# The mLSTM's full-precision products become three rounded passes each, its first decay weights are made earlier, and the local branch's rounded weights come by casting transfers

## The chip, the core and the metric

The kernel runs on one core of one Trainium2 chip. The core has five engines with an instruction queue each: TensorE (PE, matrix products; its loads of the stationary operand are listed as PEld), VectorE (DVE), ScalarE (ACT), GpSimd (POOL) and SyncE (SP). SP and POOL also issue the transfers (DMA) between the chip's memory and the core's on-chip buffers. The engines run side by side and wait for each other through semaphores.

Some results are kept in memory for later: gd (gates), god (the sigmoid of the output gates) and xk and s, into which transfers add.

The metric is the device time of one execution in microseconds (us). The kernel before takes 880.09 us, the median of three runs (879.93 to 880.3).

## The reference, cut to what matters

One decoder layer for 512 tokens of width 1024, in float32:

```python
h = rmsnorm(x, norm_mix_g)
proj = h @ w_in
qk_ml, v_ml, o_ml, if_pre, q_sw, k_sw, v_sw, g_a, g_b = split(proj)
qk_ml = silu(causal_depthwise_conv(qk_ml, conv_qk))
q_ml, k_ml = split(qk_ml)                    # 4 heads, 128 wide; q_ml is scaled by 128 ** -0.5
ig, lf = gates[..., :4], log_sigmoid(gates[..., 4:])
h_ml = mlstm_chunkwise(q_ml, k_ml, v_ml, ig, lf)      # values 256 wide
y_a = sigmoid(o_ml) * (rmsnorm_per_head(h_ml) * mlstm_norm_g)
y_b = swa_with_sinks(q_sw, k_sw, v_sw, sinks)         # 16 query heads, 4 key heads, window 128
merged = sigmoid(g_a) * (y_a @ w_branch_a) + sigmoid(g_b) * (y_b @ w_branch_b)
x = x + merged @ w_out
x = x + square(relu(rmsnorm(x, norm_mlp_g) @ w_up)) @ w_down
gate = sigmoid(rmsnorm(x, norm_ple_g) @ w_ple_gate)
x = x + gate * (p @ w_ple_proj)
return rmsnorm(x, final_norm_g)
```

The reference walks the mLSTM in chunks of 64 tokens. The kernel computes the same in one piece for each head. With b the running sum of lf and m the running maximum that keeps the exponentials in range, a token t takes from an earlier token s the weight (q_t . k_s) exp(b_t - b_s + i_s - m_t). Its numerator is the sum of these weights times v_s, its denominator the sum of the weights alone, which is found as one more column of ones behind the values.

## The kernel before, in words

**Rounded pairs.** Nearly all products are made from pairs. A float32 operand is split in a rounded half (tag wh for weights, written by an ACT cast, L137) and a remainder (wl, by a DVE subtraction, L138). Three products of halves then stand for one of full precision: high x high, high x low, low x high (`pairs`). They are issued by `chain` at L171. In the trace such products have the type f32 as the full-precision ones do, which are the exception in this kernel and are made at other lines, among them the mLSTM's scores (L819) and its output (L831).

**Weights.** `load_raw` (L152) fetches 512 KB of a weight matrix by a transfer that SP issues, into one of four wr buffers. `load_w` splits them into one of four wh and one of four wl buffers. A buffer of a tag is used in rotation: the split of a weight waits until PE has finished the weight four before it. The other pools rotate in the same way: "act" has 34 tiles of 128x512, "lm" has 4 tiles of 128x1024, "big" has 2 tiles of 128x4096, and the banks that PE writes to come as two of each tag (psg, pst, psa).

**Order.** A scheduler of the framework places the instructions of each engine, from dependencies and its own costs; `tc.issue_after` pins some of them behind a given instruction. The numbers behind names (wh_828, gg_866) are those that the scheduler's listing gives to tiles. They differ between the two kernels for the same tile.

**The stages around the change.** The front of the program forms the normalised input, the projections of the window attention, and then the mLSTM's values (`by_tokens(w_vml, ...)`) and output gates (`by_tokens(w_o, ...)`). The scheme of `by_tokens` is one of seven products of half-size blocks in place of eight; sums of weight blocks (wr, wq; L458, L462) and sums of results (L507, L510) are made beside it by ACT and DVE. `put_v` writes the values to the four tiles vm (L521, L523). Beside these products run the gates of the mLSTM: ig and fg, lf = log sigmoid, the running maximum mst (a scan, L546) and running sums fl (L549), rr = fl - mst (L551, sent to memory and read back as rows across all partitions), gg (L558, L560) and em = exp(-mst) (L562, which follows a load of ACT's table of functions). PE then turns gg and em from rows into columns (gc) by transposes at L572 and L574.

Much later, behind the window attention, `qk_proj(7)` makes the last q and k projection, and `silu` finishes the q and k of the four heads. The stage that the change rewrites then goes through the heads: `branch_b(h)` multiplies the window attention's result yb by a block of w_branch_b (24 products at L171; these blocks are called w_b[0] to w_b[7]), `ml_decay` makes the next head's exponentials (dg by DVE, ten exponentials by ACT at L802 into four tiles dm), `ml_out` forms the output of a head (L831, ten blocks of 128x128 against 257 columns) with copies hs (L834) and hd (L835) out of the banks, and `ml_scores` the next head's scores (L819, blocks of 512, 384, 256 and 128 columns), which DVE multiplies by dm (L823). `ml_norm` normalises, and `ya_of` turns the result and splits it into ya, which w_branch_a multiplies next. w_b[4] to w_b[7] alternate with `ya_of`.

## Time and profile before

| what | value |
|---|---|
| median of three runs | 880.09 us (879.93 to 880.3) |
| the profiled execution's own time | 879.82 us |
| its span | 878.0 us |
| PE busy | 866.8 us (99%), 4372 instructions |
| DVE busy | 657.2 us (75%), 966 instructions |
| ACT busy | 483.5 us (55%), 803 instructions |
| POOL busy | 34.1 us (4%), 58 instructions |
| PE's share of the chain that ended last | 90% |

The span runs from the first to the last instruction that the profile shows, and the execution's own time holds some 1.8 us more. In the view in order of time, a row gives a start in the span, a duration, the engine, the line, the operation with output and inputs, and how many instructions of one kind it puts together; products overlap in the pipeline, so starts, and not durations, tell what one costs. The row of a stretch gives the busy time of PE, PEld, DVE, ACT and POOL with the number of instructions, then the granted clock, the share of time in which transfers ran, and GB/s. The order of the program's rows, shown under the change, gives no times.

### The profile page before, as it was taken

The page shows a single profiled execution, that of the slowest core. Times are in us where ns is not written, and L with a number is a line of the kernel's source. Part 1 is how long each engine was busy: PE and PEld are TensorE (multiplying, and loading weights), DVE is VectorE, ACT ScalarE, POOL GpSimd, SP SyncE. Part 2 cuts the span into 40 slices and gives each one's busy share as a digit, 9 for nine tenths or more (in the row PEclk, how much of TensorE's full clock was granted, in tenths as well). Part 3 has the DMA queues.
Part 4 walks back from the last instruction along what each step waited for, and adds up shares of the span by engine and source line. Part 5 has one row for each costly group of instructions (what it writes and reads, how often), then busy time and mean ns, then how long its engine had stood idle before and what let it go on. Part 6 is the DMA issues. An engine that isn't in the chain of part 4 may idle for free.

```text
span 878.0 us, 11545 instructions
## 1 busy us (share of the span) xinstructions
PE 866.8 (99%) x4372; PEld 725.6 (83%) x4372; DVE 657.2 (75%) x966; ACT 483.5 (55%) x803; POOL 34.1 (4%) x58
## 2 busy tenths in 40 slices
PE   8999999999999999999999999999999999999996
PEld 7888889998777777788888888888888888888886
DVE  6999887875789876665896669756956794698557
ACT  6684554544676768743344665356435634564843
POOL 1111010000000000000020000000000000020000
PEclk9999999999999999999999999999999999999999
DMA  7765244435122162274244612530352054125302
GB/s 266 211 180 186 73 150 169 165 111 196 52 73 72 49 199 88 97 240 144 72 75 145 236 49 71 197 106 10 124 185 75 1 186 149 49 52 141 121 0 96
DMA packets 32793, 106.74 MB, mean 122 GB/s; under 512 B 4573, under 2 KB 4573, under 8 KB 32738
## 3 DMA queue, kind: packets, MB, share of 16 engines
q1 hardware_dynamic: 27570, 93.15, 31.2%
q0 software_dynamic: 5024, 12.59, 5.9%
q8 instruction: 34, 0.56, 0.3%
q10 hardware_dynamic: 144, 0.26, 0.1%
q14 instruction: 21, 0.17, 0.1%
HBM read 91.30 MB, written 8.40 MB: 114 GB/s over the span
## 4 chain that ended last, share of the span: by engine, by line
PE 90%; DVE 4%; ACT 3%; DMA 2%; issue 1%; SPq 0%; ACTq 0%; DVEq 0%
PE psg L171 50%; PE psp L171 23%; PE psa L171 7%; PE pst L171 4%; PE psa L831 1%; PE pst L747 1%; DVE wl L138 1%; DMA wr<-in_w_vsif 1%; ACT lm L712 1%; PE psa L819 1%; PE psa L689 1%; PE psa L690 1%; ACT wh L137 0%; DMA wr<-in_w_gb 0%; PE psp L980 0%
## 5 line engine op out<-in xcount | busy, mean ns | idle before, releaser
L137 ACT CAST wh<-wr 128x1024 fp32r<-128x1024 f32 x138 | 144.8, 1051 | 180.3 <-PE psg L171 74.8
L138 DVE TENSOR_TENSOR wl<-wr,wh 128x1024 fp32r<-128x1024 f32 x138 | 167.8, 1219 | 85.9 <-ACT wh L137 84.6
L171 PE MATMUL psg<-x,wh 128*128 128x512 f32 x512 | 157.7, 389 | 0.0
L171 PE MATMUL psp<-wh,uf 128*128 128x512 f32 x448 | 138.6, 389 | 0.0
L171 PEld LDWEIGHTS psg<-x,wh 128*128 128x128 f32 x512 | 96.0, 188 | 19.9
L171 PE MATMUL psg<-x,wl 128*128 128x512 f32 x256 | 99.6, 389 | 0.0
L171 PEld LDWEIGHTS psp<-wh,uf 128*128 128x128 f32 x448 | 84.1, 188 | 17.5
L171 PE MATMUL psp<-wl,uf 128*128 128x512 f32 x224 | 87.2, 389 | 0.0
L171 PE MATMUL psg<-h,wh 128*128 128x512 f32 x256 | 81.1, 395 | 0.7 <-DVE rc L715 0.7
L137 ACT CAST wh<-wd 128x1024 fp32r<-128x1024 f32 x44 | 46.2, 1052 | 54.0 <-PE psp L171 21.9
L138 DVE TENSOR_TENSOR wl<-wd,wh 128x1024 fp32r<-128x1024 f32 x44 | 53.1, 1217 | 14.7 <-ACT wh L137 14.5
L171 PEld LDWEIGHTS psg<-x,wl 128*128 128x128 f32 x256 | 48.0, 188 | 10.0
L171 PEld LDWEIGHTS psg<-h,wh 128*128 128x128 f32 x256 | 47.0, 188 | 11.2 <-issue 1.6
L171 PE MATMUL psg<-h,wl 128*128 128x512 f32 x128 | 50.5, 395 | 0.0
L138 DVE TENSOR_TENSOR uf<-F,uf 128x1792 fp32r<-128x1792 f32 (+2 forms) x20 | 33.0, 1652 | 21.8 <-ACT uf L137 21.8
L171 PEld LDWEIGHTS psp<-wl,uf 128*128 128x128 f32 x224 | 42.0, 188 | 8.7
L171 PE MATMUL psg<-yb,wh 128*128 128x512 f32 x128 | 41.3, 402 | 0.1
L171 PE MATMUL psg<-ya,wh 128*128 128x512 f32 x128 | 39.5, 390 | 0.0
L137 ACT CAST uf<-F 128x1792 fp32r<-128x1792 f32 (+2 forms) x20 | 27.9, 1396 | 20.5 <-DVE F L1133 20.4
L1157 DVE SCALAR_TENSOR_TENSOR xk<-psp,r,xk 128x512 f32<-128x512 f32 x48 | 33.7, 744 | 5.5 <-PE psp L171 5.2
L171 PE MATMUL psg<-hS,wh 128*128 128x256 f32 x192 | 35.6, 284 | 0.0
L171 PE MATMUL psa<-h,wh 128*128 128x256 f32 x192 | 35.3, 285 | 0.2 <-ACT p L625 0.2
(322 smaller groups left out, 1745.6 us busy)
## 6 DMA issues: line engine op xcount, KB each, us to landing
wr<-in_w_up SPq DMA_DIRECT2D x32, 512.0 KB, 3.3
wd<-in_w_down SPq DMA_DIRECT2D x24, 512.0 KB, 3.7
wr<-in_w_qsw SPq DMA_DIRECT2D x8, 512.0 KB, 4.3
gd<-gr POOLq DMA_DIRECT2D x8, 512.0 KB, 3.7
wr<-in_w_qkml SPq DMA_DIRECT2D x8, 512.0 KB, 3.2
wr<-in_w_b SPq DMA_DIRECT2D x8, 512.0 KB, 3.2
gl<-gd SPq DMA_DIRECT2D x8, 512.0 KB, 3.4
wr<-in_w_a SPq DMA_DIRECT2D x8, 512.0 KB, 4.4
```

The source lines that it names most:

```text
L137: A.copy(dst[0], src)
L138: last_low[0] = V.tensor_sub(dst[1], src, r32(dst[0]))
L171: last_mm[0] = T.matmul(ps, l, r, start=first and i == 0, stop=last and i == len(ops) - 1, skip_group_check=parts)
L689: T.matmul(o, q[:, n * P : (n + 1) * P], kk[kp][ab][:, k0 : k0 + 256], start=True, stop=False)
L690: T.matmul(o, q[:, n * P : (n + 1) * P], kl[kp][ab][:, k0 : k0 + 256], start=False, stop=True)
L712: A.activation(lm3[:, g, :], lm3[:, g, :], AF.Exp, bias=nmx[:, g : g + 1], scale=0.125, accum_out=sm[:, g : g + 1])
L747: T.matmul(o[HALF[ab], :], v[:, c : c + 64], w[:, ab * 512 : (ab + 1) * 512], start=j == 0, stop=j == len(terms) - 1)
L819: T.matmul(psc, qk[4 + h][:, n0 : n0 + P], qk[h][:, n0:], start=True, stop=True, skip_group_check=True)
L831: last_mm[0] = T.matmul(pn[:, t % 2, : DV + 1], wT[s][:, t * P : (t + 1) * P], vm[s][:, h, :], start=s == 0, stop=s == t, skip_group_check ...
L1157: V.scalar_tensor_tensor(o, ps[:, t, :], r2[:, 2 * toks + t : 2 * toks + t + 1], o, ALU.mult, ALU.add)
```

## The change

Four edits are made together.

1. Scores and output products of the mLSTM are made from rounded pairs. q and k of each head are split (`qk_parts`) into slots of the two big tiles that later hold ya (`spare`); the weights wT, now packed into three tiles dm, are multiplied by the scores and split too. vm becomes a rounded tile with 258 columns a head, whose two columns of ones ACT writes. `put_v` also makes the values' remainders vl by a DVE subtraction and sends them to memory (vld) by a POOL transfer; SP reads a head's remainders back into an "lm" tile before its output. The score block of the last 128 keys is formed with 256 columns, of which 128 are used. Where a result of `by_tokens` needs a sum before it is a value, the sum is now made into its own tile (L530), then cast to vm by ACT and subtracted (L532).
2. `ml_decay(0)` stands ahead of `qk_proj(7)`, and only head 0's `silu` stands ahead of its scores; the other heads' follow them.
3. The rounded half of w_b comes straight from memory by a transfer that POOL issues and that casts on the way (L161). SP still fetches the plain block, and DVE still subtracts (L162). ACT no longer casts these eight blocks.
4. Two blocks of w_b stand ahead of head 0's output, one more between head 2's output and head 3's scores, and one each with `ya_of(0)` and `ya_of(2)`.

```diff
     def tk(n):
-        return tp_.tile([P, NH * (DV + 1)], F32, tag="tk", bufs=4, name=nm(n))
+        return tp_.tile([P, NH * (DV + 2)], F32, tag="tk", bufs=4, name=nm(n))
...
-    def load_w(src, n, dims, raw=None):
+    def load_w(src, n, dims, raw=None, cast=False):
...
-        split(parts, raw[:, :n])
+        if cast:
+            nc.gpsimd.dma_start(out=parts[0], in_=src)
+            last_low[0] = V.tensor_sub(parts[1], raw[:, :n], r32(parts[0]))
+        else:
+            split(parts, raw[:, :n])
...
-        t = tk("vm").rearrange("p (h d) -> p h d", h=NH)
-        G.memset(t[:, :, DV : DV + 1], 1.0)
+        t = tp_.tile([P, NH * (DV + 2)], F32R, tag="tk", bufs=4, name=nm("vm")).rearrange("p (h d) -> p h d", h=NH)
+        A.copy(t[:, :, DV:], ones[:, : 2 * NH].rearrange("p (h d) -> p h d", h=NH))
         vm.append(t)
+    vld = dp.tile([P, NH, NT, DV], F32, name="vld")
...
     def put_v(m, nh, ps, k):
         o = vm[m][:, 2 * nh : 2 * nh + 2, :DV]
-        src = ps.rearrange("p (h d) -> p h d", h=2)
+        two = lambda t: t.rearrange("p (h d) -> p h d", h=2)
+        low = act_r("vl")
         if k is None:
-            A.copy(o, src)
+            A.copy(o, two(ps))
+            V.tensor_sub(two(low), two(ps), r32(o))
         else:
-            V.tensor_add(o, src, k.rearrange("p (h d) -> p h d", h=2))
+            V.tensor_add(k, ps, k)
+            A.copy(o, two(k))
+            V.tensor_sub(two(low), two(k), r32(o))
+        nc.gpsimd.dma_start(out=vld[:, 2 * nh : 2 * nh + 2, m, :], in_=two(r32(low)))
...
-    qk_proj(7)
-
-    for h in range(NH):
-        silu(h)
-        silu(4 + h)
-
+    ya_parts, ya = big_hl("ya")
+    turn = [0]
+    def spare():
+        k = turn[0] % KT
+        turn[0] += 1
+        return [t[:, k, :] for t in ya_parts]
+
+    def qk_parts(h):
+        for i in (h, 4 + h):
+            hl = spare()
+            split(hl, qk[i])
+            qk[i] = hl
...
+        dm = [act_f("dm") for _ in range(3)]
+        wT = [dm[0], dm[1][:, :384], dm[2][:, :256], dm[2][:, 256:384]]
...
-        banks = [two[:, :512], two[:, 512:], one, two[:, 512:]]
-        at = [0, 0, 0, 384]
-        for s in (0, 1, 3, 2):
-            n0 = s * P
-            psc = banks[s][:, at[s] : at[s] + S - n0]
-            T.matmul(psc, qk[4 + h][:, n0 : n0 + P], qk[h][:, n0:], start=True, stop=True, skip_group_check=True)
+        psc = [two[:, :512], two[:, 512:896], one[:, :256], one[:, 256:]]
+        q, k = qk[h], qk[4 + h]
         for s in range(NT):
-            n0 = s * P
-            dm = wts[h][s]
-            V.tensor_mul(dm[:, n0:], banks[s][:, at[s] : at[s] + S - n0], dm[:, n0:])
+            n0 = min(s, 2) * P
+            ops = pairs([t[:, s * P : (s + 1) * P] for t in k], [t[:, n0:] for t in q])
+            for j, (l, r) in enumerate(ops):
+                T.matmul(psc[s], l, r, start=j == 0, stop=j == 2, skip_group_check=True)
+        dm, wT = wts[h]
+        hl = []
+        for j, n in enumerate((512, 384, 384)):
+            for s in ((0,), (1,), (2, 3))[j]:
+                V.tensor_mul(wT[s], psc[s][:, P:] if s == 3 else psc[s], wT[s])
+            hl.append([t[:, :n] for t in spare()])
+            split(hl[j], dm[j][:, :n])
+        wts[h] = hl + [[t[:, 256:] for t in hl[2]]]
...
+        low = sp.tile([P, NT, DV], F32R, tag="lm", bufs=LMB, name=nm("vl"))
+        nc.sync.dma_start(out=r32(low), in_=vld[:, h])
...
-                    last_mm[0] = T.matmul(
-                        pn[:, t % 2, : DV + 1], wT[s][:, t * P : (t + 1) * P], vm[s][:, h, :], start=s == 0, stop=s == t, skip_group_check=True
-                    )
+                    hi, lo = [q[:, (t - s) * P : (t - s + 1) * P] for q in wT[s]]
+                    o = pn[:, t % 2, : DV + 2]
+                    T.matmul(o, hi, vm[s][:, h, :], start=s == 0, stop=False, skip_group_check=True)
+                    T.matmul(o[:, :DV], hi, low[:, s, :], start=False, stop=False, skip_group_check=True)
+                    last_mm[0] = T.matmul(o, lo, vm[s][:, h, :], start=False, stop=s == t, skip_group_check=True)
...
-        mm_T(ps, load_w(w_b[i], KT * P, KT), yb)
+        mm_T(ps, load_w(w_b[i], KT * P, KT, cast=True), yb)
...
     ml_decay(0)
+    qk_proj(7)
+    silu(0)
+    silu(4)
+    qk_parts(0)
     ml_scores(0)
+    for h in range(1, NH):
+        silu(h)
+        silu(4 + h)
     rds = []
+    todo = list(range(KT))
     for h in range(NH):
-        branch_b(h)
+        for _ in range(1 if h else 2):
+            branch_b(todo.pop(0))
         if h + 1 < NH:
             ml_decay(h + 1)
+            qk_parts(h + 1)
         with tc.issue_after(last_mm[0].ins):
             rds.append(ml_out(h))
         if h + 1 < NH:
+            if h == 2:
+                branch_b(todo.pop(0))
             with tc.issue_after(last_mm[0].ins):
                 ml_scores(h + 1)
...
     for h in range(NH):
-        branch_b(NH + h)
+        if h % 2 == 0:
+            branch_b(todo.pop(0))
         ya_of(h)
```

Three places in the new order are spoken of below.

The first is in the front of the program, on PE: the transposes of the gates, gg (L572) and em (L574) into a psa bank. Before, they stand between the last product of wh_828 and the first of wh_929; wl_829 is the remainder of wh_828, and h the stationary or moving halves of the input:

```order
L171 MATMUL psa_563<-wl_829,h_158 128x512
L171 MATMUL psa_563<-wh_828,h_159 128x512
L572 MATMUL psa_538<-ident,gg_866 128x4
L574 MATMUL psa_538<-ident,em_877 128x4
L572 MATMUL psa_538<-ident,gg_867 128x4 x2
L574 MATMUL psa_538<-ident,em_877 128x4
L572 MATMUL psa_538<-ident,gg_868 128x4 x3
L574 MATMUL psa_538<-ident,em_877 128x4
L572 MATMUL psa_538<-ident,gg_869 128x4 x4
L574 MATMUL psa_538<-ident,em_877 128x4
L171 MATMUL pst_925<-wh_929,h_158 128x512
```

In the changed kernel, PE has there (these lines are L582 and L584 now, and wh_976 is the block of output gates that was wh_828, wh_1000 the one that was wh_929):

```order
L175 MATMUL pst_957<-wh_976,h_159 128x512
L175 MATMUL psg_958<-wh_1039,hS_387 128x512
L175 MATMUL psg_959<-wh_1039,hS_387 128x512
L582 MATMUL psa_539<-ident,gg_897 128x4
L584 MATMUL psa_539<-ident,em_908 128x4
L582 MATMUL psa_539<-ident,gg_898 128x4 x2
L584 MATMUL psa_539<-ident,em_908 128x4
L582 MATMUL psa_539<-ident,gg_899 128x4 x3
L584 MATMUL psa_539<-ident,em_908 128x4
L582 MATMUL psa_539<-ident,gg_900 128x4 x4
L584 MATMUL psa_539<-ident,em_908 128x4
L175 MATMUL pst_956<-wh_1000,h_158 128x512
```

The transposes now stand behind the first two products of another block, wh_1039, and the product that follows them is still one of the input h.

On DVE the operations that feed these transposes stand so in the changed kernel (L530 and L532 are `put_v`, L453 a sum of weight blocks, L556 the scan that makes mst and is printed as SCALAR_TENSOR_TENSOR, L561 rr, L568 the first rows of gg):

```order
L530 TENSOR_TENSOR t_134_711<-psa_564,t_134_711 128x512
L530 TENSOR_TENSOR t_135_713<-psa_564,t_135_713 128x512
L453 TENSOR_TENSOR wr_941<-wq_945,wr_941 128x1024
L532 TENSOR_TENSOR vl_867<-t_134_711,vm_530 128x512
L532 TENSOR_TENSOR vl_872<-t_135_713,vm_532 128x512
L556 SCALAR_TENSOR_TENSOR mst_886<-lf_881,ig_877 4x512
L138 TENSOR_TENSOR wl_1001<-wr_947,wh_1000 128x1024
L561 TENSOR_TENSOR rr_893<-fl_888,mst_886 4x512
L568 TENSOR_TENSOR gg_897<-ig_877,fl_888 4x128
L568 TENSOR_TENSOR gg_898<-ig_877,fl_888 4x128
```

The two remainders vl and the scan stand ahead of the remainder wl_1001, and gg behind it. ACT's casts wh_1000 and wh_1057, of weights too, stand ahead of em in its queue, and em's instruction waits for the transfer of vl_867 too, since the tiles of the act pool rotate. wl_794 is a weight's remainder that DVE makes some 30 instructions earlier.

The second place is on DVE, while PE forms the first products of the values. Before, wl_688, wl_709 and wl_725 are remainders of weights, L462 is a sum of weight blocks, and t_132 and t_133 (L510) are sums of results, which read the banks psg that PE writes next:

```order
L138 TENSOR_TENSOR wl_688<-wr_549,wh_687 128x1024
L462 TENSOR_TENSOR wr_549<-wq_561,wr_549 128x1024
L138 TENSOR_TENSOR wl_709<-wr_547,wh_708 128x1024
L510 TENSOR_TENSOR t_132_704<-psg_566,p_112_600 128x512
L138 TENSOR_TENSOR wl_725<-wr_549,wh_724 128x1024
L510 TENSOR_TENSOR t_133_706<-psg_567,p_113_602 128x512
L138 TENSOR_TENSOR wl_745<-wq_551,wh_744 128x1024
```

In the changed kernel the same tiles are wl_695, wl_716, wl_732, t_134 and t_135:

```order
L528 TENSOR_TENSOR vl_667<-pst_565,vm_534 128x512
L138 TENSOR_TENSOR wl_695<-wr_550,wh_694 128x1024
L528 TENSOR_TENSOR vl_671<-pst_566,vm_536 128x512
L466 TENSOR_TENSOR wr_550<-wq_562,wr_550 128x1024
L138 TENSOR_TENSOR wl_716<-wr_548,wh_715 128x1024
L515 TENSOR_TENSOR t_134_711<-psg_567,p_112_601 128x512
L515 TENSOR_TENSOR t_135_713<-psg_568,p_113_603 128x512
L138 TENSOR_TENSOR wl_732<-wr_550,wh_731 128x1024
```

Two remainders of values (L528, out of the pst banks) now stand among them, ahead of t_134 and t_135, and t_135 stands ahead of the third remainder.

The third place is on DVE in the mLSTM's stage, around head 1's output, in the changed kernel. ya is a slot that holds a half of q, k or the weights, dg and dm belong to a head's weights, wl_4042 is the remainder of the seventh block of w_b, whose rounded half wh_4041 comes by the casting transfer, and hd is the column of denominators of a head:

```order
L891 TENSOR_TENSOR gb_3663<-psg_3632,gl_3664 128x512
L138 TENSOR_TENSOR ya_3359<-dm_3544,ya_3358 128x384
L810 TENSOR_TENSOR dg_3667<-row_912,tri 128x512
L162 TENSOR_TENSOR wl_4042<-wr_4039,wh_4041 128x1024
L843 TENSOR_TENSOR dm_3671<-pst_3735,dm_3671 128x256
L862 COPY hd<-psa_3688 128x2
L843 TENSOR_TENSOR dm_3671<-pst_3735,dm_3671 128x128
L862 COPY hd<-psa_3712 128x2
```

The subtraction for wl_4042 stands ahead of two multiplications by dm and of the first copy of hd; before, the remainders of w_b waited in the same queue for a cast by ACT.

More of the change, by code (lines that the diff above doesn't have):

```diff
@@ L796, in ml_decay @@
         )
-        wT = []
+        dm = [act_f("dm") for _ in range(3)]
+        wT = [dm[0], dm[1][:, :384], dm[2][:, :256], dm[2][:, 256:384]]
         for s in range(NT):
-            dm = act_f("dm")
             for t in range(s, NT):
@@ L802, in ml_decay @@
                 A.activation(
-                    dm[:, t * P : (t + 1) * P],
+                    wT[s][:, (t - s) * P : (t - s + 1) * P],
                     src[:, t * P : (t + 1) * P],
```

4 lines of the change are left out of this document (1 added, 3 removed).

## The prediction

> **What bounds the kernel now.** I read the page first, its shares and the chain that ended last, then the busy time by stretch, then each engine's rows in order of time around the edits.
>
> ```profile
> span 878.0 us, 11545 instructions
> PE 866.8 (99%) x4372; PEld 725.6 (83%) x4372; DVE 657.2 (75%) x966; ACT 483.5 (55%) x803; POOL 34.1 (4%) x58
> PE 90%; DVE 4%; ACT 3%; DMA 2%; issue 1%; SPq 0%; ACTq 0%; DVEq 0%
> ```
>
> TensorE (PE) is busy for 99% of the span and makes 90% of the chain: the time moves only if PE's products get cheaper or PE is made to wait. In the front of the program VectorE (DVE) is as full as PE:
>
> ```profile
> 65.00:70.00 5.00, 5.00 (x24) 4.14 (x23) 5.00 (x8) 2.21 (x3) 0.00 (x0) 1.00 0.95 323
> ...
> 85.00:90.00 5.00, 5.00 (x24) 4.14 (x23) 5.00 (x6) 2.48 (x4) 0.00 (x0) 1.00 0.00 0
> ...
> 100.00:105.00 5.00, 5.00 (x24) 4.14 (x23) 3.26 (x4) 2.10 (x2) 0.00 (x0) 1.00 0.33 102
> ```
>
> The columns are PE, PEld, DVE, ACT, POOL. All five stretches from 65 to 90 us have DVE at 5.00 of 5.00; room returns by 100. So work added to DVE before 90 us has no cover there but the weights prepared ahead.
>
> **1. The products of the mLSTM.** Prices of PE, as starts of rows:
>
> ```profile
> 149.99 0.40 PE L171 MATMUL psg<-hS,wh 128*128 128x256 f32 x2
> 150.23 0.28 PE L171 MATMUL psg<-hS,wl 128*128 128x256 f32 x1
> ...
> 343.76 0.45 PE pst L819 x2
> ...
> 366.75 1.72 PE psa L819 x6
> ...
> 369.85 4.33 PE psa L831 x20
> ...
> 380.55 5.46 PE psg L171 x24
> ```
>
> Rounded products start every 5.46/24 = 0.2275 us at 512 columns, and two of 256 columns take 150.23 - 149.99 = 0.24, so 0.12 each. On the line between them (an estimate) 258 columns cost 0.121 and 384 cost 0.174. Full-precision products show as two records each.
> - Before, a head: scores 1.72 + 0.43, output 4.33, together 6.48; four heads 25.9 us.
> - After, a head: scores 3 x 0.2275 + 3 x 0.174 + 6 x 0.12 = 1.925 (the fourth block is widened to 256 columns); output 10 x (0.121 + 0.120 + 0.121) = 3.62; four heads 22.2 us.
>
> The gain on PE is 3.7 us. [...] Here the loads take as long as this:
>
> ```profile
> L171 PEld LDWEIGHTS psg<-hS,wh x192: 186/192/193, 124.4 to 200.5; 128*128 128x128 f32 x192
> ```
>
> The row's loads of 192 ns stand under products that start every 120 ns, so several overlap. [...]
>
> **2. Waits of that stage.** It runs from w_b[0] to w_b[4]:
>
> ```profile
> 325.23 0.63 PE L171 MATMUL psg<-yb,wh 128*128 128x512 f32 x2
> ...
> 329.81 0.40 PE L171 MATMUL psg<-yb,wl 128*128 128x512 f32 x1
> 330.35 0.96 PE L171 MATMUL psg<-yb,wh 128*128 128x512 f32 x3
> ...
> 373.83 0.81 PE L171 MATMUL psg<-yb,wh 128*128 128x512 f32 x2
> ```
>
> 373.83 - 325.23 = 48.6 us, less 96 x 0.2275 = 21.8 and the heads' 25.9, leaves 0.85 us of waits (0.54 - 0.23 = 0.3 of it at 329.81). That one waits for yb casts which stand on ACT behind the sigmoid's table load; in the changed order they stand ahead of it, and a whole w_b weight follows before the scores. I take all 0.85 as gained. Walking the changed order through this stage by hand, I find head 0's rounded weights ready near 336.0 and wanted by the output at 338.1; head 1's second block is ready about 0.2 us late (ACT does squares between its casts): +0.2.
>
> Splits of q, k and the weights add to DVE 8 x 0.6 + 4 x 1.5 = 11 us, and to ACT about 10 us, from which the eight w_b casts of 1.05 us fall away. What hides them:
>
> ```profile
> 325.00:330.00 5.00, 5.00 (x23) 3.87 (x21) 3.81 (x8) 4.78 (x8) 0.00 (x0) 1.00 0.85 311
> ...
> 370.00:375.00 5.00, 5.00 (x25) 4.31 (x24) 4.04 (x10) 3.46 (x5) 0.00 (x0) 1.00 0.65 184
> ```
>
> Over these ten stretches DVE is busy 33.6 of 50 us and ACT 41.1, so after it 44 to 45 and 43. It fits, with little to spare. The exponentials of head 0 (10 x 0.29 us) cost nothing where they now stand, between yb evictions, while ACT waits for PE.
>
> **3. Casting transfers.** No row casts. The nearest:
>
> ```profile
> gd<-gr POOLq DMA_DIRECT2D x8, 512.0 KB, 3.7
> hS<-s POOLq DMA_DIRECT2D x8, 256.0 KB, 4.4
> xk<-q POOLq DMA_DIRECT2D x6, 256.0 KB, 5.5
> god<-t POOLq DMA_DIRECT2D x4, 256.0 KB, 2.7
> ```
>
> Plain from POOL: 3.7 us for the size; accumulating, half the size takes 4.4 to 5.5, or 1.7 to 2.8 more than plain. If casting slowed each byte as accumulating does, 512 KB would take 3.7 + 2 x 1.7 = 7.1 us or more. I take 3.7, the same size; the ends are 3.2 and 9.3. Each transfer waits for PE to release the buffer four weights earlier. The tight one is w_b[6]: released near 349.1, issued 349.3, landed 353.0, while DVE reaches its subtraction at 351.0 and stands. Behind it are the next head's blocks and the copy of hd that frees the bank for head 2's scores: 353.0 + 1.13 + 0.5 = 354.7 against PE's need at 354.5. Cost 0.3 us with the wake-up. [...]
>
> **4. Remainders of the values, in the full stretch.** put_v gains eight subtractions of 512 columns. The intervals of DVE:
>
> ```profile
> 58.45 1.22 DVE L138 TENSOR_TENSOR wl<-wr,wh 128x1024 fp32r<-128x1024 f32 x1
> ...
> 59.58 0.68 DVE L510 TENSOR_TENSOR t<-psg,p 128x512 f32<-128x512 f32 x1
> ...
> 64.38 0.67 DVE L544 SCALAR_TENSOR_TENSOR lf<-fg,lf 4x512 f32<-4x512 f32 x1
> 64.98 0.67 DVE L510 TENSOR_TENSOR t<-psg,p 128x512 f32<-128x512 f32 x1
> ...
> 68.44 1.21 DVE L546 TENSOR_TENSOR_SCAN mst<-lf,ig 4x512 f32<-4x512 f32 x1
> 69.58 1.33 DVE L549 TENSOR_TENSOR_SCAN fl<-lf,zero 4x128 f32<-4x128 f32 x4
> 70.84 1.19 DVE L138 TENSOR_TENSOR wl<-wr,wh 128x1024 fp32r<-128x1024 f32 x1
> ```
>
> 1.13 us for a wl or a 1024-wide sum, 0.60 for 512 columns, 1.14 and 1.26 for the scans.
>
> (a) vl_671 goes ahead of the addition t_134, which frees the bank for the next products. Two casts of vm by ACT push wh_694 from 56.02 to 56.3; then wl 1.13, vl 0.60, sum 1.14, wl 1.13: t_134 starts at 60.35, ends 61.03, PE goes on at 61.08. Before, it went on at 60.52 (in 60.29 + 0.2275):
>
> ```profile
> 60.29 0.62 PE L171 MATMUL psg<-wh,hS 128*128 128x512 f32 x2
> ...
> 82.42 0.22 PE L572 MATMUL psa<-ident,gg 4*128 4x4 f32 x1
> ...
> 83.38 0.50 PE L171 MATMUL pst<-wh,h 128*128 128x512 f32 x1
> ```
>
> +0.56 us.
>
> (b) The transposes of gg and em stand later in PE's order, behind the first two products of wh_1039, and gg is made later by DVE, behind vl_872, the scan mst and wl_1001. From wl_794 (65.4, when its half from ACT is there) to the last gg DVE has 7 wl, 4 sums, 16 operations of 512, the two scans and 1.7 us of gg: 7.9 + 4.6 + 9.6 + 2.4 + 1.7 = 26.2, so 91.6. em ends there too. Its rows:
>
> ```profile
> 77.09 1.06 ACT L137 CAST wh<-wr 128x1024 fp32r<-128x1024 f32 x1 [1.66 <-PE psg L171]
> 78.17 1.28 ACT L562 ACT_TABLE_LOAD   x1
> 79.56 0.63 ACT L562 ACTIVATE em<-mst 4x512 f32<-4x512 f32 x1
> ```
>
> wh_1057 is ahead of it on ACT and needs PE to finish wh_976 at 88.4: 88.6 + 1.06 + 1.28 + 0.63 = 91.6. em also waits for vl_867's transfer: started about 86.8, 2.7 us as god, 89.5, in time. PE is there at 61.08 + 122 x 0.2275 = 88.85. Its transposes then go on from 91.65 and take about 0.85, to 92.5: 3.65 us where they took 83.38 - 82.42 = 0.96. +2.7 us. Behind them everything on PE waits; nothing later gives it back, since PE has no slack. The weights after it are again early by more than 1 us.
>
> **Sum.** -3.7 - 0.85 + 0.2 + 0.3 + 0.56 + 2.7 = -0.8 us. The profiled execution took 879.82 us, 0.27 under the median of 880.09 and 1.8 over its span; taken from the median, 879.3 us, a span near 877.2.
>
> **Rivals.**
> 1. The front covers it: the transposes are not late, and only the gain stays. For it: weights there are ready 5 us early in many places (wh at 77.09 serves PE at 86.24). Against: the two sums of (b) meet at 91.6 on different engines. Then -0.8 - 3.3 = -4.1: 876.0 us.
> 2. Slow casts, the other side. At 5.5 us w_b[6] holds DVE until 354.8, PE 1.8 us longer, and w_b[5] (released 338.1, wanted by DVE at 343.1) 0.5 longer: 881.6. At 7.1 it is about 4 and 2 more: 885. It decides from 4.5 us on; at 6 us the whole is slower by over 0.2%. For it: accumulating rows; against: a cast reads no second operand.
> 3. The front waits longer: vl_867 lands after 5.5 us, as the xk rows do, not 2.7; em and PE 2.6 us later: 881.9.
> 4. Short products paced by their loads at 0.19 us: 42 x 0.19 x 4 = 31.9 instead of 22.2, +9.7: 889. [...]
>
> **How the numbers follow.** About 0.2% (1.76 us) is what a measurement of this kernel tells from no change. Forecast 0.44, its own range 878.2 to 880.8; rival 1 0.18, rival 2 0.20, rival 3 0.10, rival 4 0.02, others 0.06. Faster: rival 1 and the forecast's low end, 0.27. Slower: most of rivals 2 to 4, 0.29. Same: 0.44. The range 875.8 to 882.4 holds rivals 1 and 3 and the nearer half of 2.
>
> **What would show it.** Twenty-four rounded w_b products at 5.46 and a head's output at 3.6 us on PE (1); no wait at the first w_b (2); DVE idle until a transfer wh<-in_w_b before the seventh wl of w_b (3); PE idle about 0.5 near 60.5 and 2.8 near 89, released by em or gg (4). It is wrong if PE passes 89 without a wait, or if casting transfers land after more than 4.5 us.

## The result, and the profile after

The changed kernel takes 883.55 us (median of six runs, 882.83 to 884.35), the kernel before 880.28 us on the same chip (six runs, 879.93 to 880.91). The ratio is 1.0038, with a 95% interval of 1.0026 to 1.005: slower, by 3.3 us. The prediction said 879.3 and at most 882.4. The profiled execution took 883.39 us with a span of 881.5, 3.5 longer than the span before. One execution among those of the experiments (of e7: 957.12 us, at a mean granted clock of 0.849) is slow as a whole and is left out of all medians and ratios.

The page of the changed kernel, its span and engines:

```profile
span 881.5 us, 11736 instructions
PE 866.3 (98%) x4428; PEld 728.9 (83%) x4428; DVE 672.0 (76%) x994; ACT 488.8 (55%) x825; POOL 43.8 (5%) x70
```

PE is busy 0.5 us less than before in a span that is 3.5 us longer. A share of busy time can't say why; the rows in order of time can. I follow a few marks on PE from before to after, each the start of the first product of the same block: behind the sum t (60.52 before), the attention branch in the middle of the program, and the second block of w_branch_a behind the mLSTM. The marks of before, then of after:

```profile
317.10 0.71 PE L171 MATMUL psg<-h,wh 128*128 128x512 f32 x2
...
404.85 0.61 PE L171 MATMUL psg<-ya,wh 128*128 128x512 f32 x2
```

```profile
60.97 0.47 PE L175 MATMUL psg<-wh,hS 128*128 128x512 f32 x1 [0.28 <-DVE t L515]
...
324.09 0.71 PE L175 MATMUL psg<-h,wh 128*128 128x512 f32 x2
...
408.33 0.61 PE L175 MATMUL psg<-ya,wh 128*128 128x512 f32 x2
```

The changed kernel is 0.45 us late at the first mark, 6.99 at the second and 3.48 at the third. The mLSTM stage between the last two gained 3.5 us. So some 6.5 us were lost between 61 and 324 us, and PE's rows in order of time show nearly all of it around the transposes of the gates. The bracket at the end of a row is the idle time ahead of it and what ended it:

```profile
88.27 0.61 PE L175 MATMUL psg<-wh,hS 128*128 128x512 f32 x2
90.91 0.22 PE L582 MATMUL psa<-ident,gg 4*128 4x4 f32 x1 [2.02 <-DVE gg L568]
92.02 0.22 PE L584 MATMUL psa<-ident,em 4*128 4x4 f32 x1 [0.88 <-ACT em L572]
...
93.20 0.80 PE L175 MATMUL pst<-wh,h 128*128 128x512 f32 x1
93.80 0.63 PE L175 MATMUL pst<-wl,h 128*128 128x512 f32 x1
94.22 1.05 PE L175 MATMUL pst<-wh,h 128*128 128x512 f32 x2
...
99.32 0.62 PE L175 MATMUL pst<-wh,h 128*128 128x512 f32 x2
```

Two things are lost here. First the wait: the last product ahead ends its turn at 88.27 + 2 x 0.2275 = 88.73, the next product starts at 93.20, so the transposes hold PE for 4.48 us where they held it for 1.04 (from 82.11 + 0.2275 to 83.38): +3.44. Second, the products behind the wait: from 93.20 to 99.32 us fourteen of them start, one every 0.437 us, where 0.2275 is the price: +2.9 us. The stretches of the same kernel (PE, PEld, DVE, ACT and POOL busy, granted clock, DMA share, GB/s) show that as the clock, the sixth figure behind the stretch's length:

```profile
89.00:90.00 1.00, 0.00 (x0) 0.00 (x0) 1.00 (x2) 0.56 (x1) 0.00 (x0) 1.00 0.81 328
...
93.00:94.00 1.00, 1.00 (x5) 0.89 (x5) 1.00 (x7) 0.00 (x0) 0.99 (x2) 0.50 0.00 0
...
98.00:99.00 1.00, 1.00 (x4) 0.74 (x3) 1.00 (x2) 0.00 (x0) 0.00 (x0) 0.50 0.23 78
...
100.00:101.00 1.00, 1.00 (x6) 0.82 (x5) 0.72 (x1) 0.53 (x1) 0.00 (x0) 1.00 0.00 0
```

Here the clock is 1.00 while PE stands idle, falls to 0.50 at 92.4, one and a half microseconds after the first transpose and 0.4 after the end of the second wait, and is back at 99.3, 6.8 us later. PE counts as fully busy in these stretches; only the clock and the count of PE's instructions (4 between 98 and 99, 6 between 100 and 101) give the loss away. 0.45 + 3.44 + 2.9 = 6.8 of the 6.99 us.

What PE waits for stands on two engines. First DVE, then ACT:

```profile
86.53 1.29 DVE L532 TENSOR_TENSOR vl<-t,vm 128x512 fp32r<-128x512 f32 x2
87.73 1.20 DVE L556 TENSOR_TENSOR_SCAN mst<-lf,ig 4x512 f32<-4x512 f32 x1
88.86 1.19 DVE L138 TENSOR_TENSOR wl<-wr,wh 128x1024 fp32r<-128x1024 f32 x1
89.98 0.67 DVE L561 TENSOR_TENSOR rr<-fl,mst 4x512 f32<-4x512 f32 x1
90.58 0.47 DVE L568 TENSOR_TENSOR gg<-ig,fl 4x128 f32<-4x128 f32 x2
```

```profile
90.04 1.28 ACT L572 ACT_TABLE_LOAD   x1 [0.48 <-DMA vld<-vl]
91.33 0.63 ACT L572 ACTIVATE em<-mst 4x512 f32<-4x512 f32 x1
```

DVE works without a gap and reaches gg at 90.6 us. ACT waits until 90.04 for the transfer of a remainder vl, whose act tile em takes over, and em is there at 91.96.

### The profile page after: what moved, and what is told of

It reads as the page before. It is cut to its first block, busy times and chain, and to the rows that moved or that the text cites. A ratio compares the mean times of both kernels' runs of the same rounds, so it can differ in the third digit from the quotient of the medians.

```text
span 881.5 us, 11736 instructions
## 1 busy us (share of the span) xinstructions
PE 866.3 (98%) x4428; PEld 728.9 (83%) x4428; DVE 672.0 (76%) x994; ACT 488.8 (55%) x825; POOL 43.8 (5%) x70
## 4 chain that ended last, share of the span: by engine, by line
PE 68%; issue 3%; DVE 3%; ACT 2%; DMA 0%; POOL 0%; POOLq 0%; ACTq 0%
PE psg L175 39%; PE psp L175 23%; PE pst L757 1%; PE psa L175 1%; ACT lm L722 1%; PE psa L699 1%; PE psa L700 1%; DVE wl L138 0%; PE psp L1017 0%; PE psa L736 0%; DMA wh<-in_w_b 0%; PE psp L1025 0%; DVE qs L429 0%; ACT wh L137 0%; PE pst L898 0%
## 5 line engine op out<-in xcount | busy, mean ns | idle before, releaser
L137 ACT CAST wh<-wr 128x1024 fp32r<-128x1024 f32 x130 | 136.5, 1052 | 164.1 <-PE psg L175 59.8
L138 DVE TENSOR_TENSOR wl<-wr,wh 128x1024 fp32r<-128x1024 f32 x130 | 158.1, 1219 | 86.3 <-ACT wh L137 85.3
```

The costliest lines, as they stand in the source:

```text
L137: A.copy(dst[0], src)
L138: last_low[0] = V.tensor_sub(dst[1], src, r32(dst[0]))
```

## The experiments

Two theories stood at the start. By the first, the clock: PE's wait halves the granted clock behind it, and this costs about as much as the wait itself. By the second, the load: the slow products are slow by what DVE, ACT and the transfers do beside them, and the wait alone is the cost. Beneath both lay the question what makes gg and em late. Ratios are to the kernel before, run on the same chip, with 95% intervals.

### e1: the transposes 26 products later

```diff
-    pgc = pg[:, :512]
-    with tc.issue_after(last_mm[0].ins):
...
+    def gate_cols():
+        pgc = pg[:, :512]
+        with tc.issue_after(last_mm[0].ins):
...
-    by_tokens(w_o, post_by_tokens(put_o))
+    by_tokens(w_o, post_by_tokens(put_o), cols=gate_cols)
```

The transposes are written inside the output gates, behind the product group that `by_tokens` calls c11.

> The changed kernel with the gate transposes (gg, em) moved 26 products later on PE, behind the fourth block of the output gates; DVE's and ACT's queues keep their order. Theory (idle PE halves its own clock): no wait of 2.9 us near 89 us and no stretch at clock 0.50, about 1 us of waiting left because the remainder wl_1001 now ends some 1 us after PE wants it; 883.5 - 3.4 - 3.0 + 1.1 = 878.2 us. Rival A (the half clock between 93 and 99 us has another cause, such as the load of all engines there): the wait goes, the half clock stays; 881.2 us. Rival B (DVE is simply too full): the wait moves to the next weights undiminished; 883 us.

Measured: 883.85 us, 1.0042 (1.0027 to 1.0057). The wait for gg and em is gone, and a new one has taken its place. PE's row, and the stretch around it:

```profile
92.58 0.69 PE L175 MATMUL pst<-wh,h 128*128 128x512 f32 x1 [3.71 <-ACT p L524]
```

```profile
92.00:96.00 4.00, 3.42 (x8) 2.70 (x9) 4.00 (x6) 2.29 (x4) 2.16 (x4) 0.59 0.32 97
```

The next block's products need a bank that ACT empties with a copy p, and p stands in ACT's queue behind em, which still waits for the remainder's transfer. So taking away PE's direct wait on em was not enough: em blocks ACT, and ACT blocks PE. I had not followed who stands behind em in ACT's queue. The half clock came here too, from 92.72 to 96.14 us. The outcome is rival B's: the wait moved and did not get shorter.

### e2, e3 and e7: filling the wait with useless products

The transposes are pinned to one place in PE's order, behind 24 products of the output gates. e2 does this alone; e3 puts 13 products, whose result nobody reads, right ahead of them, e7 puts 6.

```diff
+    def gate_cols(wf, xf):
+        pgc = pg[:, :512]
+        for _ in range(13):
+            with tc.issue_after(last_mm[0].ins):
+                last_mm[0] = T.matmul(pg[:, 512:].rearrange("p (h d) -> p h d", h=2), wf, xf, start=True, stop=True, skip_group_check=True)
+        with tc.issue_after(last_mm[0].ins):
...
-    by_tokens(w_o, post_by_tokens(put_o))
+    by_tokens(w_o, post_by_tokens(put_o), cols=gate_cols)
```

> The changed kernel with the transposes pinned by hand where the scheduler had put them (behind the first 24 products of the output gates, with the two products of wh_1039 behind them). A base for the next run: a wait of 3.3 us instead of 2.9, the same half clock after it, 883.5 us within 0.5 under every theory.

> The base kernel with pinned transposes and 13 useless rounded products of 512 columns on PE directly ahead of them, into an unused half of the bank. They need no late data and take 13 x 0.2275 = 2.96 us, which is the time that PE waits in the base. Theory (idle PE halves its clock): PE is busy up to the transposes, waits under 0.6 us, and the clock stays at 1.00; 3.0 us faster than the base, 880.5 us, though PE does more. Rival A (the half clock has another cause): as the base, 883.5 us. Rival B (the products delay what follows): slower than the base, up to 886.5 us.

> The base with pinned transposes and 6 useless products in place of 13 ahead of them: PE waits 3.4 - 6 x 0.2275 = 2.0 us there. The order and all other work are those of the base. If any wait of 2 us is enough to halve the clock: as the base, spans of 880.3 to 882.3 us. If the wait has to be longer (the 1.2 to 1.3 us of waiting at 10 us passes at clock 1.00 in every profile): clock 1.00 and the span of the run with 13 products, 878.6 us, since the products fill time in which PE would wait.

| | useless products | median, us | ratio (95%) | profiled span, us | PE idle ahead of gg and em, us | half clock in the profiled run, us |
|---|---|---|---|---|---|---|
| e2 | 0 | 882.63 | 1.0033 (1.002 to 1.0046) | 882.3 | 2.54 + 0.89 | 6.8 |
| e7 | 6 | 882.72 | 1.0034 (1.0021 to 1.0048) | 880.9 | 1.40 + 0.89 | 3.4 |
| e3 | 13 | 881.0 | 1.0014 (1.0005 to 1.0024) | 878.6 | 0.40 (em) | none |

The stretches of e2, and then those of e3:

```profile
92.00:96.00 4.00, 3.89 (x19) 3.39 (x20) 3.92 (x10) 1.00 (x3) 2.16 (x4) 0.54 0.26 78
96.00:100.00 4.00, 4.00 (x12) 3.10 (x12) 3.97 (x5) 0.00 (x0) 0.00 (x0) 0.61 0.51 191
```

```profile
92.00:96.00 4.00, 3.98 (x27) 3.44 (x28) 4.00 (x10) 2.19 (x3) 2.16 (x4) 1.00 0.32 91
96.00:100.00 4.00, 4.00 (x19) 3.34 (x18) 3.96 (x5) 1.70 (x3) 0.93 (x2) 1.00 0.55 207
```

DVE, the transfers and the place are alike, the useless work takes 13 x 0.2275 = 2.96 us of the 3.43 us of waiting, so nothing else became shorter; yet the profiled span fell by 3.7 us and the clock stayed at 1.00 with 19 instructions of PE in the second stretch instead of 12. In these two executions it is the wait that halves the clock, and the second theory falls: DVE is as full in e3 as in e2.

The medians differ by 1.6 us only. The profiled execution of e2 is its slowest; the four others had less of the half clock (spans of 880.3 to 880.9 at a mean clock of 0.997, against 882.3 at 0.993). And of e3's ten executions three had spans of 879.8 to 880.8, without a trace that would say why, where the others had 878.4 to 879.3. e7's span went the same way: 880.0 to 880.9 at 0.997, or 882.5 and 882.6 at 0.993 to 0.995. The two groups lie 1.6 to 2.6 us apart; half of a stretch of 3.4 us is 1.7. e7 also shows how little is enough: 1.40 + 0.89 us of idle time, from two waits with a transpose between them, still brought 3.4 us of half clock, and e3's 0.40 brought none.

### e4, e10 and e11: the change without the remainders, and its other parts

```diff
-        low = act_r("vl")
...
-            V.tensor_sub(two(low), two(ps), r32(o))
...
-            V.tensor_sub(two(low), two(k), r32(o))
-        nc.gpsimd.dma_start(out=vld[:, 2 * nh : 2 * nh + 2, m, :], in_=two(r32(low)))
+        nc.gpsimd.dma_start(out=vld[:, 2 * nh : 2 * nh + 2, m, :], in_=r32(o))
```

e10 is e4 with w_b rounded by ACT again, e11 is e4 with `ml_decay(0)` back behind the other heads' `silu`:

```diff
-        mm_T(ps, load_w(w_b[i], KT * P, KT, cast=True), yb)
+        mm_T(ps, load_w(w_b[i], KT * P, KT), yb)
```

```diff
-    ml_decay(0)
     qk_proj(7)
...
         silu(4 + h)
+    ml_decay(0)
```

> The changed kernel without the eight subtractions that make the values' remainders: the rounded values themselves are sent to memory in their place, by the same eight transfers, so the output leaves the remainders out and is not the reference's. Everything else stays, the low products too. Theory (the subtractions, 8 x 0.60 us in a full DVE, make gg and em late): transposes stand and run as before the change, no wait, clock 1.00, the 0.45 us near 60.5 gone as well; 883.5 - 7.0 = 876.5 us. Rival C (the transfers of the remainders, or the casts of the values by ACT, make them late): the wait stays at 2 us or more; 881 to 883.5 us.

> The run without the subtractions, and the rounded half of w_b cast by ACT again (the casting transfers undone). The base takes 876.6 us; in the changed kernel's profile DVE waited 1.93 us for one casting transfer and PE 0.3 us after it. If that was the transfers' whole effect: 876.3 us. If ACT needs the 8 x 1.05 us that it gets back (busy 43 of 50 us in the mLSTM's stage by the prediction's sum): rounded weights or the next head's blocks late, 877.5 to 879 us.

> The run without the subtractions, and head 0's ten exponentials again behind the last projection of q and k (ml_decay(0) moved back). If their place costs and brings nothing, as the prediction has it: 876.6 us within 0.4. If they had been on the path to the first scores, they are 10 x 0.29 = 2.9 us on ACT: up to 879.5 us, with PE waiting at the first blocks of w_b or at the scores.

Measured: e4 876.63 us, 0.9964 (0.9951 to 0.9977), span 874.8; e10 876.23, 0.9955 (0.994 to 0.9969), span 874.6; e11 877.91, 0.9973 (0.9963 to 0.9983), span 875.2. Without the eight subtractions PE reaches the transposes without a wait, as e4's row shows (no bracket, so no idle time ahead):

```profile
82.49 0.22 PE L579 MATMUL psa<-ident,gg 4*128 4x4 f32 x1
```

Each against the kernel before on its own chip, the changed kernel is 3.3 us slower and e4 3.4 us faster (880.0 before). So the eight subtractions, with the tiles that they write, cost 6.6 us, where their own time on DVE is 8 x 0.6 = 4.8, and all the rest of the change is worth some 3.4. The casting transfers cost 0.4 us by medians and 0.2 by the profiled spans, which the overlapping intervals of e4 and e10 do not tell from nothing. The early exponentials are worth 1.3 us by medians and 0.4 by the profiled spans (the profiled execution of e11 is its fastest). With them back, the first block of w_b still runs without a wait; PE waits at the third, behind head 0's output, in e11:

```profile
343.02 0.74 PE L175 MATMUL psg<-yb,wh 128*128 128x512 f32 x2 [0.43 <-DVE gb L888]
```

### e5 and e6: the remainders in place, by DVE and by POOL

Six of the eight remainders are written over the sum they are made from, so they need no act tile. e6 has POOL subtract.

```diff
-            V.tensor_sub(two(low), two(k), r32(o))
-        nc.gpsimd.dma_start(out=vld[:, 2 * nh : 2 * nh + 2, m, :], in_=two(r32(low)))
+            G.tensor_sub(two(k), two(k), r32(o))
+            low = k
+        nc.gpsimd.dma_start(out=vld[:, 2 * nh : 2 * nh + 2, m, :], in_=two(low if k is not None else r32(low)))
```

> The changed kernel with six of the eight remainders of the values made in place, in the tile of the sum, and no tile of their own. DVE does the same work; only the act pool has six tiles less in rotation, and the scheduler places the scan mst and gg earlier. Theory (DVE's work is what is late): the wait moves from the transposes to the remainder of the output gates' third block, which now has mst, rr and gg ahead of it: about 3 us of waiting near 90 us, half clock after it, 882.5 to 884 us. Rival D (tiles that are not free, not DVE, make gg and em late): no wait over 1 us, clock 1.00, 877 to 878 us.

> As the run before, and the six subtractions are made by POOL, which takes 3.6 us from DVE between 75 and 92 us. Nothing needs them before 340 us. Theory (DVE's work is what is late): wait near 90 us under 1 us, clock 1.00 throughout; 883.5 - 3.4 - 3.0 + 0.5 = 877.6 us, faster than before the change. Rival E (POOL's subtractions slow DVE's own instructions beside them by as much as they save): DVE's 1.13 us remainders become longer there, and the time stays above 880 us.

e5 took 882.0 us, 1.002 (1.0011 to 1.0029). gg is in time there, em is not: it stands behind casts of vm that wait for DVE's sum t. ACT's rows, with PE's wait behind them:

```profile
85.36 1.22 ACT L531 CAST vm<-t 128x512 fp32r<-128x512 f32 x2 [1.23 <-DVE t L530]
86.59 1.28 ACT L573 ACT_TABLE_LOAD   x1
87.89 0.63 ACT L573 ACTIVATE em<-mst 4x512 f32<-4x512 f32 x1
```

```profile
88.57 0.22 PE L585 MATMUL psa<-ident,em 4*128 4x4 f32 x1 [2.49 <-ACT em L573]
```

One wait of 2.49 us, and again 3.4 us of half clock, from 89.42 to 92.84. The time is near the 882.5 to 884 expected, but the place is not: the wait was expected at a remainder of weights behind mst, rr and gg on DVE, and it is em, behind DVE's sum t, that is late.

e6 took 885.78 us, 1.0062 (1.0047 to 1.0077): moving the work off the full engine made the program slower. POOL's rows, and then DVE's:

```profile
76.00 2.05 POOL L532 TENSOR_TENSOR t<-t,vm 128x512 f32<-128x512 f32 x1 [16.36 <-ACT vm L531]
...
83.38 2.35 POOL L532 TENSOR_TENSOR p<-p,vm 128x512 f32<-128x512 f32 x2
```

```profile
76.91 1.67 DVE L562 TENSOR_TENSOR rr<-fl,mst 4x512 f32<-4x512 f32 x1
...
83.84 2.04 DVE L569 TENSOR_TENSOR gg<-ig,fl 4x128 f32<-4x128 f32 x1 [0.77 <-DMA vld<-t]
...
89.48 1.27 DVE L530 TENSOR_TENSOR t<-psa,t 128x512 f32<-128x512 f32 x2
```

rr takes 0.67 us in the changed kernel and 1.67 here, and ends 0.53 us after POOL's subtraction does; one gg takes 2.04 against 0.27, and ends 0.15 us after a pair of POOL's subtractions. So in e6 these two operations of DVE stand while POOL subtracts. PE then waits 5.62 us for em, which stands in ACT's queue behind a cast of the sum t. That sum starts at 89.48, 4.8 us later than in e5 (84.65). The two stretched operations are 2.8 us of DVE's time; besides, three operations on weights (from 86.07 to 89.48, 3.4 us) now stand ahead of t, which in e5 follow it. How the 4.8 us divide between the two, no run shows.

### e8 and e9: is it DVE's work, or the tiles?

e8 takes the subtractions out of the front (the unrounded values go to memory, and at some 200 us a head's values are read back, subtracted and written again). e9 keeps them in the front but gives their results two tiles of another pool, so that em waits for no transfer. Both pin em's place on ACT.

```diff
+        nc.sync.dma_start(out=r32(low), in_=vld[:, h])
+        for m in range(NT):
+            V.tensor_sub(low[:, m, :], r32(low[:, m, :]), r32(vm[m][:, h, :DV]))
+        nc.gpsimd.dma_start(out=vld[:, h], in_=r32(low))
```

```diff
-        low = act_r("vl")
+        low = sp.tile([P, 1024], F32R, tag="pT", bufs=2, name=nm("vl"))[:, :512]
```

> The changed kernel with the remainders of the values taken out of the front: the full values go to memory by the same eight transfers, and after the last gate projection, near 200 to 230 us, where DVE is busy 4.4 to 6.7 of 10 us, SP reads each head back, DVE subtracts (16 operations of 256 columns) and POOL writes the remainders. em is pinned ahead of the cast of the output gates' third block. Nothing is left out. Theory (the eight subtractions and their tiles make the front wait): as the run without subtractions, no wait near 82 to 92 us, clock 1.00, 876.7 us, faster than both kernels. Rival F (the front stays late because of ACT's eight casts of the values, which are still there, or the 16 subtractions make PE wait near 210 us): 878 to 881 us.

> The changed kernel with all eight subtractions on DVE in the front, but their results in two tiles of another pool, which stand empty there, so the act pool is as before the change; em pinned ahead of the cast of the output gates' second block. The transposes then stand where they stood before the change. Theory DVE's work (4.8 us more before the output gates' third block): transposes and em in time within 0.5 us, but the remainder of the third block (wl_1001) ends near 91.3 us where PE wants it at 89.4: a wait of 1 to 2.5 us, 878 to 880 us. Theory tiles (the act pool's rotation made everything late): no wait over 0.5 us, 876.8 us.

e8 took 891.38 us, 1.0129 (1.0111 to 1.0147). Even with no subtraction in the front, em is late, because its tile still waits for a transfer of values; ACT's row, then PE's:

```profile
84.16 1.28 ACT L576 ACT_TABLE_LOAD   x1 [3.92 <-DMA vld<-p]
```

```profile
86.14 0.22 PE L588 MATMUL psa<-ident,em 4*128 4x4 f32 x1 [3.44 <-ACT em L576]
...
225.64 1.19 PE L175 MATMUL psg<-h,wh 128*128 128x512 f32 x2 [5.26 <-DVE qs L429]
```

DVE then stands for 6.34 us until 220.03, where the late subtractions wait for their reads to land, PE waits 5.26 us, and each of the two waits has its own stretch of half clock (3.4 us from 87.22, 6.8 from 223.74). Most of what e8 loses is that second place; for the question it shows only that the tile's rotation is enough by itself to make em late.

e9 took 880.99 us, 1.0011 (1.0001 to 1.002), span 878.7, clock 1.00 through the whole front. PE's waits are many and short:

```profile
58.64 0.50 PE L175 MATMUL psg<-wl,hS 128*128 128x512 f32 x1 [0.44 <-DVE wl L138]
...
62.32 0.47 PE L175 MATMUL psg<-wh,hS 128*128 128x512 f32 x1 [0.90 <-DVE t L521]
...
91.81 0.73 PE L175 MATMUL psg<-wh,hS 128*128 128x512 f32 x2 [0.53 <-ACT wh L137]
```

At the first product of the window attention's scores (220.04 us before), PE is 4.36 us late in e9, 6.96 in the changed kernel and 0.20 in e4. So with the same eight subtractions PE loses 4.2 us in waits under a microsecond that leave the clock alone, and 2.6 us less than in the changed kernel, where PE waits for 2.02 and 0.88 us around one transpose and the clock falls to 0.50.

The 4.2 us are not the price of DVE's work alone, and e9 fits neither of its expectations (no wait of 1 us or more, and yet 880.99). The expectation took the two tiles to be empty in the front, and they are not; DVE's row for the first remainder:

```profile
56.76 0.69 DVE L534 TENSOR_TENSOR vl<-pst,vm 128x512 fp32r<-128x512 f32 x1 [1.64 <-DMA hS<-s]
```

It stands 1.64 us until a transfer out of the tile's former use has landed, and another remainder stands 0.76 us, until 81.74, for the transfer of a remainder. Behind the sum t PE is already 1.80 us late in e9 (62.32 against 60.52), where it is 0.45 late in the changed kernel. So DVE's work (in the changed kernel it runs without a gap from 74 us to gg) and tiles that wait for transfers (e8) both make the front late; how the 6.8 us divide between them stays open.

### e12: a version that beats both

Nothing is left out. The values go to memory as they are; behind the gates' projections, where ACT has room, ACT makes the negative of the rounded values, and a transfer adds it in memory. em has a tile of another pool, and w_b is rounded by ACT as before.

```diff
-            V.tensor_sub(two(low), two(k), r32(o))
-        nc.gpsimd.dma_start(out=vld[:, 2 * nh : 2 * nh + 2, m, :], in_=two(r32(low)))
+        nc.gpsimd.dma_start(out=vld[:, 2 * nh : 2 * nh + 2, m, :], in_=two(k))
...
+    for m in range(NT):
+        neg = sp.tile([P, NH, DV], F32, tag="pT", bufs=2, name=nm("neg"))
+        A.activation(neg, vm[m][:, :, :DV], AF.Copy, scale=-1.0)
+        nc.gpsimd.dma_start(out=vld[:, :, m, :], in_=neg, accum_op=ALU.add)
```

> Nothing left out, and neither DVE's work nor the tiles in the front: the full values go to memory by eight transfers; ACT makes the negative of the rounded values behind the last gate projection (4 x about 1.05 us, where it is busy 3.7 to 5.1 of 10 us), and POOL's transfers add it in memory, which leaves the remainders there. em gets a tile of the pool that stands empty there, so it waits for no transfer. The casting transfers of w_b are undone as well. Theory (the front is late by DVE's 4.8 us and by tiles that wait for transfers, and by nothing else of the change): no wait of PE over 0.5 us between 55 and 100 us, clock 1.00, 876.23 us as the run without subtractions and without casting transfers, within 0.6; faster than both kernels. Rival G (gg's tiles still wait for the transfers, or the two more copies of values on ACT are late): a wait of 2 us or more near 82 us and a stretch at half clock, 880 to 884 us.

Measured: 878.11 us against 880.1 before, 0.9976 (0.9967 to 0.9986); span 876.6. It is 2.0 us faster than the kernel before and 5.4 faster than the changed one. Its rows:

```profile
82.47 0.22 PE L580 MATMUL psa<-ident,gg 4*128 4x4 f32 x1
89.66 0.50 PE L175 MATMUL pst<-wh,h 128*128 128x512 f32 x1 [0.49 <-ACT p L512]
...
203.66 0.47 PE L175 MATMUL psa<-h,wh 128*128 128x256 f32 x2 [0.71 <-DVE t L627]
```

The transposes come without a wait, and the clock stays at 1.00 until PE has finished. It misses its expectation by 1.9 us; the two waits shown are 1.2 of that, the second of them right behind the time in which ACT makes the negatives (189.6 to 200.7). What rival G named is there in small: two gg still wait for transfers of values, 0.34 and 0.57 us on DVE.

## Why the prediction was wrong, point by point

**The step that failed is 4 (b), in what it left out.** It gave the wait for gg and em +2.7 us and took everything behind it at full price ("the weights after it are again early"). The places and causes were as it said: gg at the end of a full DVE, em on ACT behind a table load. The wait itself came out at +3.44, 0.7 more: the remainder's transfer, taken to land at 89.5 and in time, landed at 90.04 and held ACT for 0.48 us, so that em ended at 91.96 and not 91.6, and the transposes behind em took 1.18 us and not 0.85, most of that time at the lowered clock. Missing altogether was the price of the products behind the wait: fourteen at half clock, +2.9 us. e2 against e3 shows that the idle time of PE is the cause. With these two figures and the stage as measured, the sum is 0.45 + 3.44 + 2.9 - 3.5 = +3.3, and the measured difference is +3.3 (+3.5 by the spans). The range's upper end held a later transfer or slow casts, and no longer price behind a wait that it had itself forecast.

**1, the products: right.** The output of a head and the scores of the next, each with the first product behind it:

```profile
367.66 0.28 PE L858 MATMUL psa<-vm,ya 128*128 128x258 f32 x1
...
371.26 0.62 PE L175 MATMUL psg<-yb,wh 128*128 128x512 f32 x2
...
376.70 0.39 PE L838 MATMUL psa<-ya 128*128 128x512 f32 x1
...
378.63 0.63 PE L175 MATMUL psg<-yb,wh 128*128 128x512 f32 x2
```

3.60 us (predicted 3.62) and 1.93 (1.925). Thirty short products a head at 0.12 us each, under loads of 187 to 192 ns, decide against rival 4.

**2, the waits of the stage: mostly right.** The first w_b block now runs without a wait, its 24 products from 332.22 to 337.69. The exponentials' new place, to which the prediction gave no price, has one: put back, they cost 0.4 to 1.3 us (e11), though not at this block. The 0.2 for head 1 was not seen. The stage gained 3.5 us, not 4.05; one wait that I had not foreseen stands in front of the last blocks, where `ya_of` needs a split of DVE:

```profile
396.79 0.65 PE L898 MATMUL pst<-ident,hs 128*128 128x128 f32 x4 [0.27 <-DVE ya L141]
```

The product ahead of it starts at 396.14, so it costs 0.65 - 0.23 = 0.4 us. What else is short of the forecast, some 0.4 us, I can't place.

**3, the casting transfers: right.** The page gives their landing, and DVE's row is the predicted one, the seventh w_b block:

```profile
wh<-in_w_b POOLq DMA_DIRECT2D x8, 512.0 KB, 3.8
```

```profile
360.07 1.22 DVE L162 TENSOR_TENSOR wl<-wr,wh 128x1024 fp32r<-128x1024 f32 x1 [1.93 <-DMA wh<-in_w_b]
```

3.8 us to landing against 3.7 forecast, DVE idle until the transfer, and 0.3 us on PE (the next scores start at 361.75, where the product ahead ends its turn at 361.25 + 0.2275); e10 gives 0.4 by medians for all eight. The cast cost this transfer 0.1 us against the plain gd row of before, 0.4 against the same row in the changed kernel (3.4), and rival 2 falls.

**4 (a): right.** PE goes on at 60.97, 0.45 us later than before, where 0.56 was forecast.

**The rivals.** Rival 1, a front that covers the subtractions, did not occur; its 876.0 is near what e4 takes with a front that has none (876.63). Rival 3 did not occur: the remainder's transfer landed half a microsecond later than forecast, not 2.6.

## What to carry to other kernels

Where the profile shows an engine with no room, added work can cost its full time and more (6.6 us here for 4.8 us of subtractions), and it is best given to an engine or a transfer at another place, as in e12, not to POOL beside it, as in e6 (885.78 us against 882.0 with DVE in e5). A wait of TensorE can cost more than itself: here every wait of some two microseconds and more did, by 3.4 or 6.8 us of half clock behind it or around it, so price the products that run there at about twice their time (0.437 us for 0.2275 here), and split or fill such waits where they can't be removed. Ask of each tile that rotates not only who writes it but which transfer holds it, and of each blocked instruction who stands behind it in its queue.

## What the runs showed of the hardware

**The clock of TensorE after a wait.** Apart from the end of the program, where PE has finished, half-clock stretches had one of two lengths: 3.4 us (e1, e5, e7, the front of e8) or 6.8 us (the changed kernel, e2, e6 near 91 us, e8 from 223.74). They begin up to some 1.5 us after the end of the last wait, or while PE still stands: 1.3 us ahead of its next instruction in e6, 1.9 in e8's second. These belong to waits of 2.3 to 5.6 us, and none to those of 0.9 us and less in e9. One more stretch shows that the length of the wait is not all. In e6's profile the clock is at half from 12.94 to 16.36 us, behind a wait of 1.23 us:

```profile
12.89 1.90 PE L315 MATMUL psa<-ident,xn 128*128 128x128 f32 x8 [1.23 <-DVE xn L304]
```

The same wait, of 0.58 to 1.34 us, left the clock at 1.00 in every other profile. The shortest waits ahead of a fall were one of 2.49 us (e5), two of 1.40 and 0.89 (e7) and one of 1.23 (e6). Executions of one kernel differ too: the two groups of e7 lie 1.6 to 2.6 us apart in span. How long PE must stand for the clock to fall, and what sets the length of a stretch, no run shows.

**POOL and DVE.** All in e6: a subtraction of 512 columns took POOL 1.2 us (two in 2.35 at 83.38, one in 1.20 at 94.73; 0.60 on DVE). Three took longer, each with an operation of DVE on two tiles beside it: 2.05 at 76.00, where a remainder of DVE runs until 76.98, 1.68 at 79.10 (a remainder until 79.72) and 2.57 at 90.89 (a sum of weight blocks until 92.42). In the same way three of DVE's operations on two tiles took longer, and ended behind a subtraction of POOL: rr 1.67 us instead of 0.67 (0.53 us behind it), a gg 2.04 instead of 0.27 (0.15), a remainder of weights 2.25 instead of 1.21 (94.77; 1.09). Two sums of DVE with one input in a bank of PE did not take longer beside POOL's subtraction of 79.10 (1.27 us at 79.65, and 1.27 at 89.48 with no subtraction beside them). Why they hold each other up, no run shows.

**Transfers.** 512 KB cast on the way took 3.8 us to landing from POOL, about as plain ones did (gd from POOL: 3.7 before, 3.4 in the changed kernel; the plain blocks of w_b from SP: 3.2 and 3.3); the issue took 0.53 us of POOL's time.
